# Two-layer block on one core: where the first norm's convolution taps, its gate and the local means are computed

## The chip, the cores and the metric

One core of one Trainium2 chip runs the whole program in one launch. The metric is device time in microseconds (us). Five engines run their own instruction queues in order: TensorE (PE for its products, PEld for its weight loads), VectorE (DVE), ScalarE (ACT), GpSimd (POOL), and SyncE (SP), whose queue issues nearly all DMA transfers here. Tiles lie in SBUF; TensorE writes its results to PSUM, eight banks of 512 fp32 columns on 128 partitions.

## The reference

Two layers act on x (1024 tokens by 1024 channels). Each takes h = rms(x) scaled and shifted by vectors made from c, puts it through a mixer, and adds the mixer's result times a gate vector to x. Layer 0 mixes by convolution, layer 1 by pooling:

```
a, b, g = split(h @ w_in, 3)                  # layer 0: 1024 -> 3 x 1024
y = a * sigmoid(b)
y = depthwise_conv(y, dw, 31 taps) + db       # along the tokens
y = silu(layernorm(y, ln_g, ln_b)) * silu(g)
x = x + gate * (y @ w_out)

v, g = split(h @ w_in, 2)                     # layer 1: 1024 -> 2 x 1024
pooled = window_mean(v, 2 | 4 | 8 | 16 by channel group) - v
y = (pooled @ w_grp) * scale                  # 4 groups of 256 channels
x = x + gate * ((y * silu(g)) @ w_out)
```

Everything is fp32. The tolerance is met by splitting each operand of a large product in two fp32r parts, hi (the rounded value) and lo (the rest), and summing three products (hi x hi, hi x lo, lo x hi).

## The kernel before

Channels lie on partitions, in eight tiles of 128 (ct, kt or m); tokens on columns, in two halves of 512 (h = 0, 1). A large product of one tile and half is 24 products (`mm3`, lines 202 to 205: three for each of eight input tiles) into one bank. `load_split` loads a weight tile of 512 KB, rounds it on ScalarE (`hi_part`, line 166) and takes the rest on VectorE or GpSimd (`lo_part`, line 171).

The order of work is: norm of x and modulation; for each channel tile a, b and y; the depthwise convolution of half 0; the gates silu(g) of half 0 (`gate_g`, stored to DRAM and read back); the norm of half 0 (`layernorm`), its SiLU and gating (`gate_norm`), the output product and residual (`out_half`), the second layer's input (`h2_half`); then layer 1 for part 0 of the tokens (the first 504; the rest is part 1) in four groups of two channel tiles (`layer1_group`), while the convolution of half 1 runs; then the same chain for half 1 and part 1.

The convolution has two forms. For tiles 1 and 3 of half 0 and 1, 3, 5, 6, 7 of half 1, ScalarE multiplies the input by a tap into a tile `pr` (line 468) and GpSimd adds it (line 469), 30 adds after a seed (line 465). For the others VectorE multiplies and adds tap by tap into two banks (lines 477, 481), summed at the end. In half 1 these are tiles 0, 2 and 4, in this order.

A planner fixes the order on each engine when the program is built. It runs the program on estimated durations, takes the ready instruction of the highest priority (by default the one created first; `priority(-LATER)` moves ahead, `conv` is put far behind), and honours three written orders: `behind([i])` queues what the block creates on i's own engine behind i; `ordered` puts an instruction behind the one created before it on its engine; and tiles of one tag get their slots in the order in which the code creates them. Banks come in three tags: mm (5), ax (1), cv (2).

What the change touches:

- The four modulation vectors (`gemv`, tag ax) advance in 16 steps; 7 are called between the a and b weights of tiles 4 to 7 (`MODS[0]`), 9 after the first three gates of half 0 (`MODS[1]`).
- `layernorm(0)` sums z over channels into a bank `mr` (mm in half 0, cv in half 1), spreads the mean into `mu` (ax), subtracts it on VectorE (line 542), squares on ScalarE (272) and sums the squares with TensorE into `vpz` (274). `rstd_rows` makes the power on GpSimd (240), a diagonal on ScalarE (245) and a spread bank `rb`.
- The convolution of tile 0 of half 1 is cut in pieces: `fill` creates 2 taps behind the mean, 3 behind the last subtraction, 1 and 3 in `rstd_rows` (`GAPS`); the other 22 are queued behind the last instruction of the gating. Tile 3 is queued behind the spread of the norm. Tile 2 has 8 taps behind the gating and the others behind the last instruction of h2.
- `gate_norm` scales a tile by `rb` (564, two tiles ahead), applies SiLU in place on ScalarE (567), multiplies by the gate (559), copies the rounded value (560) and subtracts it (171), all but the SiLU on VectorE and in SBUF.
- `window_mean` (part 0 and part 1) adds the value tile `v`, a copy of the product's bank, to itself shifted (671), doubles the window (675), corrects the edge on GpSimd (684), takes mean minus value (686) and splits it (166, 171).

Of the kernel before, what the change touches and what calls it, by code (L numbers as in the profile page):

```python
# [27 lines left out]
FILL = (4, 6, 5, 7)  # L28
EARLY = 8
MIX_AT = 4  # L30
# [4 lines left out]
HOLD = (4, 2, 3, 4)  # L35
GAPS = (2, 3, 1, 3)
LAST = 2
# [6 lines left out]
AFTER = mybir.DependencyInfo(mybir.DependencyClass.NoSync, mybir.DependencyReason.DATA)  # L44
MODS = ((1, 2, 2, 2), (3, 3, 3, 0, 0, 0))
CONVS = [
# [9 lines left out]
def hybrid_kernel(ctx, tc, xT, vecs, wm, wk, cv_first, cv_w, cv_wo, pl_w, pl_grp, pl_wo, out):  # L56
# [169 lines left out]

    def rstd_rows(total, name, fill=None):


        summed, vp = total  # L230
        if summed is not None:
            vp = axps(f"vp{name}")
            with priority(-LATER):
                for j in range(4):
                    nc.tensor.matmul(vp[:, j : j + 1], summed[:, bl(j)], ones[:, 0:1], start=True, stop=True)
        ve = S.tile([P, 4], F32, tag="ve", name=f"ve{name}", bufs=2)
        with priority(-LATER):
            scaled = nc.scalar.activation(ve, vp[:, 0:4], AF.Identity, scale=1.0 / D, bias=eps)  # L238
# [8 lines left out]
        if fill is not None:  # L247
            fill(GAPS[2], scaled)
            fill(GAPS[3], spread)
        spread_done[0] = spread  # L250
        return rb, done
# [15 lines left out]
    def square_sums(xs, name, vp):  # L267


        def add(i):  # L270
            sq = half("sq", f"sq{name}{i}")
            nc.scalar.activation(sq, xs[i], AF.Square)  # L272
            for j in range(4):
                last = nc.tensor.matmul(  # L274
                    vp[:, j : j + 1], sq[:, bl(j)], ones[:, 0:1], start=i + j == 0, stop=i == KT - 1,
                    skip_group_check=True,
                )
            return last

        return (None, vp), add  # L280
# [235 lines left out]

    for i, ct in enumerate((*FILL, *CORD[:2])):
        gate_g(ct, (0,) if ct in FILL else (0, 1))
        step(MODS[1][i])
    wg_last = {ct: gate_w(ct, 0) for ct in CORD[2:4]}  # L520
    for ct in CORD[2:4]:
        gate_g(ct, (0,), wg=wg_last[ct])

    sums_done = [None, None]

    def layernorm(h, banks, fill=None):
        z = [zs[h][ct] for ct in CORD]
        sums = bank(banks, f"mr{h}")
        row = S.tile([P, HW], F32, tag="row", name=f"mrow{h}", bufs=1)
# [7 lines left out]
        sums_done[h] = last  # L537
        if fill is not None:
            fill(GAPS[0], last)
        total, add = square_sums(z, f"z{h}", bank(banks, f"vpz{h}"))  # L540
        for i in range(KT):
            sub = nc.vector.tensor_tensor(out=z[i], in0=z[i], in1=mu, op=ALU.subtract)
            with priority(-LATER):
                add(i)
        if fill is not None:
            fill(GAPS[1], sub)
        return z, *rstd_rows(total, f"z{h}", fill)

    def gate_norm(h, z, rb):
# [7 lines left out]
        for i in range(-2, KT):  # L557
            if i >= 0:
                ordered(nc.vector.tensor_tensor(out=z[i], in0=z[i], in1=gates[i // 2][:, hs(i % 2)], op=ALU.mult))  # L559
                ordered(nc.vector.tensor_copy(y1[i][0], z[i]))  # L560
                end = ordered(lo_part(*y1[i], z[i]))
            if i + 2 < KT:
                ct, v = CORD[i + 2], z[i + 2]
                mul = nc.vector.tensor_tensor(out=v, in0=v, in1=rb, op=ALU.mult)  # L564
                if i > -2:
                    ordered(mul)
                last = nc.scalar.activation(v, v, AF.Silu, scale=vcol(ct, V_LG), bias=vcol(ct, V_LB))  # L567
        return y1, [last, end]
# [98 lines left out]

    def window_mean(ct, part, v, s):
# [17 lines left out]
        nc.vector.scalar_tensor_tensor(  # L686
            out=s, in0=s, scalar=1.0 / w, in1=v[:, PAD : PAD + n], op0=ALU.mult, op1=ALU.subtract
        )
        return split_to(*hi_lo(unit(f"Z{1 + ct % 2}", f"pd{ct}{part}", F32R, 2 * lo_at[part]), part), s)

    def layer1_group(g, part, h2, early=(), prev=None):
# [189 lines left out]
```

## Time and profile before

| | us |
|---|---|
| three runs | 807.47, 809.14, 805.24 (median 807.47) |
| profiled execution | 806.57, span 804.8 |
| TensorE busy | 736.9 (92%), 3564 products |
| VectorE busy | 588.6 (73%) |
| GpSimd busy | 421.4 (52%) |
| ScalarE busy | 380.4 (47%) |
| mean granted TensorE clock | 0.962 |

Busy shares are of the whole span and hide that the engines take turns: TensorE is near 20 of 20 us from 100 to 280 us, and VectorE and GpSimd have their full stretches between 310 and 560. A wait is listed as waiter, then what it waited for; a chain of waits is read from the end back. L481 is line 481.

### The profile page before, as it was taken

The page shows a single profiled execution, that of the slowest core. Times are in us where ns is not written, and L with a number is a line of the kernel's source. Part 1 is how long each engine was busy: PE and PEld are TensorE (multiplying, and loading weights), DVE is VectorE, ACT ScalarE, POOL GpSimd, SP SyncE. Part 2 cuts the span into 40 slices and gives each one's busy share as a digit, 9 for nine tenths or more (in the row PEclk, how much of TensorE's full clock was granted, in tenths as well). Part 3 has the DMA queues.
Part 4 walks back from the last instruction along what each step waited for, and adds up shares of the span by engine and source line. Part 5 has one row for each costly group of instructions (what it writes and reads, how often), then busy time and mean ns, then how long its engine had stood idle before and what let it go on. Part 6 is the DMA issues. An engine that isn't in the chain of part 4 may idle for free.

```text
span 804.8 us, 9866 instructions
## 1 busy us (share of the span) xinstructions
PE 736.9 (92%) x3564; PEld 582.9 (72%) x3564; DVE 588.6 (73%) x754; ACT 380.4 (47%) x560; POOL 421.4 (52%) x356
## 2 busy tenths in 40 slices
PE   3999999999999997699989768998899979999998
PEld 1677787777776675478767556775778758888998
DVE  6998997999994144999789999995285562666521
ACT  5446566566433225657766665752332442333210
POOL 2001899999400004879978989996121631444322
PEclk7899999999999997999999979899999989999999
DMA  9880022434268610343631222426432540233232
GB/s 338 321 293 23 1 72 112 158 111 171 86 210 316 219 53 26 119 157 117 198 104 40 79 91 80 133 91 234 156 118 104 185 142 1 92 106 130 79 108 80
DMA packets 36481, 105.68 MB, mean 131 GB/s; under 512 B 4048, under 2 KB 6224, under 8 KB 36432
## 3 DMA queue, kind: packets, MB, share of 16 engines
q1 hardware_dynamic: 36432, 105.05, 37.9%
q8 instruction: 28, 0.46, 0.2%
q14 instruction: 21, 0.17, 0.1%
HBM read 92.45 MB, written 12.58 MB: 131 GB/s over the span
## 4 chain that ended last, share of the span: by engine, by line
PE 56%; POOL 17%; DVE 11%; issue 7%; ACT 4%; DMA 4%; SPq 0%; POOLq 0%; ACTq 0%; DVEq 0%
POOL z L469 13%; PE ps L203 4%; PE ps L205 4%; PE ps L204 4%; PE psg L203 3%; PE psg L205 3%; PE psg L204 3%; PE psf L203 2%; PE pso L204 2%; PE psf L204 2%; PE psf L205 2%; PE pso L205 2%; PE pso L203 2%; PE psq L205 2%; PE gv L296 2%
## 5 line engine op out<-in xcount | busy, mean ns | idle before, releaser
L469 POOL TENSOR_TENSOR z<-z,pr 128x512 f32<-128x512 f32 (+8 forms) x210 | 311.5, 1484 | 49.6 <-ACT pr L468 21.9
L468 ACT ACTIVATE pr<-y,VT 128x512 f32<-128x512 f32 (+8 forms) x210 | 149.7, 719 | 101.4 <-POOL z L469 97.2
L481 DVE SCALAR_TENSOR_TENSOR cv<-y,VT,cv 128x512 f32<-128x512 f32 (+15 forms) x261 | 177.5, 742 | 0.2
L240 POOL TENSOR_TENSOR vrz<-vez,mhalf 128x4 f32<-128x4 f32 x2 | 2.0, 1018 | 122.2 <-ACT vez L238 122.2
L771 DVE SCALAR_TENSOR_TENSOR xf<-psf,gt,xf 128x260 f32<-128x260 f32 (+1 forms) x24 | 13.2, 570 | 40.8 <-PE psf L205 32.2
L671 DVE TENSOR_TENSOR s<-v 128x519 f32<-128x519 f32 (+1 forms) x16 | 21.8, 1362 | 19.4 <-ACT v L720 19.4
L754 DVE SCALAR_TENSOR_TENSOR q<-psy,VT,q 128x260 f32<-128x260 f32 (+1 forms) x24 | 13.4, 569 | 26.3 <-PE psy L205 26.2
L240 POOL TENSOR_TENSOR vrx<-vex,mhalf 128x4 f32<-128x4 f32 x2 | 2.1, 1026 | 56.5 <-ACT vex L238 56.5
L564 DVE TENSOR_TENSOR z<-z,rbz 128x512 f32<-128x512 f32 x16 | 10.7, 680 | 20.6 <-PE rbz L246 20.6
L675 DVE TENSOR_TENSOR s<-s 128x517 f32<-128x517 f32 (+5 forms) x24 | 23.1, 965 | 0.2
L567 ACT ACTIVATE z<-z,VT 128x512 f32<-128x512 f32 x16 | 12.8, 814 | 21.8 <-DVE z L564 21.8
L686 DVE SCALAR_TENSOR_TENSOR s<-s,v 128x504 f32<-128x504 f32 (+1 forms) x16 | 20.6, 1290 | 3.1 <-POOL s L684 2.9
L272 ACT ACTIVATE sqz<-z 128x512 f32<-128x512 f32 x16 | 10.0, 631 | 23.9 <-PE vpz L274 18.8
L171 DVE TENSOR_TENSOR y<-q,y 128x504 fp32r<-128x504 f32 (+1 forms) x16 | 17.4, 1090 | 3.7 <-ACT y L166 3.7
L284 DVE SCALAR_TENSOR_TENSOR wmb<-wmb,s_row 128x1024 f32<-128x1024 f32 x16 | 19.4, 1224 | 0.3 <-DMA wmb<-in_wm 0.3
L274 PEld LDWEIGHTS vpz<-ones,sqz 128*128 128x128 f32 x128 | 16.6, 204 | 2.4 <-ACT sqz L272 1.8
L513 ACT ACTIVATE sgw<-psg 128x512 f32<-128x512 f32 x16 | 9.5, 592 | 18.5 <-issue 11.1
L559 DVE TENSOR_TENSOR z<-z,sgr 128x512 f32<-128x512 f32 x16 | 17.3, 1080 | 1.0 <-ACT z L567 1.0
L296 PE MATMUL gv<-wk,srep 128*32 128x256 f32 x256 | 18.0, 386 | 0.0
L171 DVE TENSOR_TENSOR pd<-s,pd 128x504 fp32r<-128x504 f32 (+1 forms) x16 | 16.3, 1028 | 2.2 <-ACT pd L166 2.1
L166 ACT CAST y<-q 128x504 fp32r<-128x504 f32 (+1 forms) x16 | 9.8, 617 | 16.9 <-DVE q L754 16.8
L166 ACT CAST pd<-s 128x504 fp32r<-128x504 f32 (+1 forms) x16 | 9.8, 618 | 16.5 <-DVE s L686 12.1
(2496 smaller groups left out, 2385.4 us busy)
## 6 DMA issues: line engine op xcount, KB each, us to landing
wk<-in_wk SPq DMA_DIRECT2D x32, 512.0 KB, 5.3
wmb<-in_wm SPq DMA_DIRECT2D x16, 512.0 KB, 6.5
wo<-in_cv_wo SPq DMA_DIRECT2D x16, 512.0 KB, 4.2
wp<-in_pl_wo SPq DMA_DIRECT2D x16, 512.0 KB, 3.4
wg<-in_cv_w SPq DMA_DIRECT2D x12, 512.0 KB, 3.3
wv<-in_pl_w SPq DMA_DIRECT2D x12, 512.0 KB, 3.4
wq<-in_pl_w SPq DMA_DIRECT2D x12, 512.0 KB, 3.4
x<-in_xT SPq DMA_DIRECT2D x16, 256.0 KB, 6.4
```

Source lines behind the costliest of these rows:

```text
L166: return nc.scalar.copy(hi, src)
L171: return eng.tensor_tensor(out=lo, in0=src, in1=hi.bitcast(F32), op=ALU.subtract)
L203: nc.tensor.matmul(ps, w[0], r[0], start=first, stop=False)
L204: nc.tensor.matmul(ps, w[0], r[1], start=False, stop=False)
L205: nc.tensor.matmul(ps, w[1], r[0], start=False, stop=last)
L296: nc.tensor.matmul(ps[32 * q : 32 * q + 32, :256], srep[:, kt, :], w[:, 256 * q : 256 * q + 256], start=kt == 0, stop=kt == KT - 1,)
L468: nc.scalar.activation(pr[:, o], y[:, i], AF.Copy, scale=dw(k))
L469: nc.gpsimd.tensor_tensor(out=z[:, o], in0=z[:, o], in1=pr[:, o], op=ALU.add)
L481: nc.vector.scalar_tensor_tensor(out=a[:, o], in0=y[:, i], scalar=dw(k), in1=a[:, o], op0=ALU.mult, op1=ALU.add)
L671: nc.vector.tensor_tensor(out=s[:, :m], in0=v[:, :m], in1=v[:, 1 : m + 1], op=ALU.add)
L675: nc.vector.tensor_tensor(out=s[:, :m], in0=s[:, :m], in1=s[:, step : step + m], op=ALU.add)
L686: nc.vector.scalar_tensor_tensor(out=s, in0=s, scalar=1.0 / w, in1=v[:, PAD : PAD + n], op0=ALU.mult, op1=ALU.subtract)
```

## The change

Four edits. (1) All 16 modulation steps run between the weights of tiles 4 to 7; the mean's bank `mr` is of tag ax in both halves. (2) The convolutions of tiles 0, 1 and 2 of half 1 are created whole behind the gating with no written order; tile 3 is queued behind the last square of half 0 and no longer behind the spread. (3) The gating writes the SiLU to a bank of tag cv, multiplies there, rounds on ScalarE and subtracts on VectorE from the bank. (4) In part 0 the window sum takes one of its two inputs from the product's bank, the mean minus value is written over that bank, and the split reads it there; GpSimd clears seven columns of the sum tile first.

```diff
-MODS = ((1, 2, 2, 2), (3, 3, 3, 0, 0, 0))
@@ for ct in range(FIRST, KT):
     wb = load_split(cv_w[KT + ct], f"wb{ct}")
-    step(MODS[0][ct - FIRST])
+    step(2)
     wa = load_split(cv_w[ct], f"wa{ct}")
+    step(2)
@@ gates of half 0
     gate_g(ct, (0,) if ct in FILL else (0, 1))
-    step(MODS[1][i])
@@ layernorm
-    sums = bank(banks, f"mr{h}")
+    sums = axps(f"mr{h}")
-    total, add = square_sums(z, f"z{h}", bank(banks, f"vpz{h}"))
+    total, add = square_sums(z, f"z{h}", bank(("mm", "cv")[h], f"vpz{h}"))
+            squared[h] = add(i)      # the last square, on ScalarE
@@ gate_norm
-            ordered(nc.vector.tensor_tensor(out=z[i], in0=z[i], in1=gates[i // 2][:, hs(i % 2)], op=ALU.mult))
-            ordered(nc.vector.tensor_copy(y1[i][0], z[i]))
-            end = ordered(lo_part(*y1[i], z[i]))
+            b = bank("cv", f"gn{h}{i}")
+            last = nc.scalar.activation(
+                b, z[i], AF.Silu, scale=vcol(CORD[i], V_LG), bias=vcol(CORD[i], V_LB)
+            )
+            ordered(nc.vector.tensor_tensor(out=b, in0=b, in1=gates[i // 2][:, hs(i % 2)], op=ALU.mult))
+            hi_part(y1[i][0], b)
+            end = ordered(lo_part(*y1[i], b))
         if i + 2 < KT:
             mul = nc.vector.tensor_tensor(out=v, in0=v, in1=rb, op=ALU.mult)
             if i > -2:
                 ordered(mul)
-            last = nc.scalar.activation(v, v, AF.Silu, scale=vcol(ct, V_LG), bias=vcol(ct, V_LB))
@@ around the first norm
-early_taps = conv_taps(1, 0)
-def fill(count, ins):
-    with behind([ins]):
-        conv(1, 0, early_taps, count)
-z, rb, rb_done = layernorm(0, "mm", fill)
+z, rb, rb_done = layernorm(0)
...
-with behind(done[1:]):
-    conv(1, 0, early_taps)
-    conv(1, 1)
-    with behind(spread_done):
-        conv(1, 3)
-    taps = conv_taps(1, 2)
-    conv(1, 2, taps, EARLY)
+conv(1, 0)
+conv(1, 1)
+with behind([squared[0]]):
+    conv(1, 3)
+conv(1, 2)
...
         with behind([h2_done]):
-            conv(1, 2, taps)
             for ct in range(4, KT):
                 conv(1, ct)
@@ window_mean(ct, part, v, s, ps)
-    nc.vector.tensor_tensor(out=s[:, :m], in0=v[:, :m], in1=v[:, 1 : m + 1], op=ALU.add)
+    if part == 0:
+        nc.gpsimd.memset(s[:, : PAD - 1], 0.0)
+        nc.vector.tensor_tensor(out=s[:, PAD - 1 : m], in0=v[:, PAD - 1 : m], in1=ps, op=ALU.add)
+    else:
+        nc.vector.tensor_tensor(out=s[:, :m], in0=v[:, :m], in1=v[:, 1 : m + 1], op=ALU.add)
...
+    res, v = (ps[:, :n],) * 2 if part == 0 else (s, v[:, PAD : PAD + n])
+    nc.vector.scalar_tensor_tensor(out=res, in0=s, scalar=1.0 / w, in1=v, op0=ALU.mult, op1=ALU.subtract)
+    return split_to(*hi_lo(unit(f"Z{1 + ct % 2}", f"pd{ct}{part}", F32R, 2 * lo_at[part]), part), res)
```

## Rows read from the trace of the kernel before

**Rows 1.** The page's chain that ended last, by line.

```profile
POOL z L469 13%; PE ps L203 4%; PE ps L205 4%; PE ps L204 4%; PE psg L203 3%; PE psg L205 3%; PE psg L204 3%; PE psf L203 2%; PE pso L204 2%; PE psf L204 2%; PE psf L205 2%; PE pso L205 2%; PE pso L203 2%; PE psq L205 2%; PE gv L296 2%
```

**Rows 2.** Busy us by stage: length, PE, PEld, DVE, ACT, POOL; clock; DMA share, GB/s.

```profile
280.00:310.00 30.00, 26.02 (x138) 21.31 (x131) 9.49 (x15) 8.59 (x17) 1.02 (x1) 0.85 0.12 44
310.00:345.00 35.00, 24.73 (x82) 15.23 (x81) 31.93 (x32) 21.83 (x32) 27.57 (x19) 0.93 0.26 83
345.00:400.00 55.00, 54.30 (x259) 44.85 (x260) 48.03 (x54) 37.97 (x58) 48.58 (x31) 0.97 0.51 168
400.00:425.00 25.00, 21.18 (x84) 14.67 (x82) 22.41 (x20) 17.67 (x28) 19.68 (x16) 1.00 0.28 94
425.00:560.00 135.00, 115.85 (x466) 89.48 (x467) 123.36 (x129) 79.08 (x117) 122.62 (x96) 0.92 0.32 105
```

**Rows 3.** TensorE's waits, 425 to 560: us in total, times, longest.

```profile
PE psv L205 <- DVE wv40l L171: 7.0, 1, 7.0
```

**Rows 4.** Timeline of TensorE: start us, duration us, line, tiles; idle before, releaser.

```profile
279.10 1.92 PE L534 MATMUL mr<-z,onesd 128*32 128x512 f32 x16
...
294.63 1.84 PE L274 MATMUL vpz<-ones,sqz 128*128 128x1 f32 x16
...
300.33 1.84 PE L274 MATMUL vpz<-ones,sqz 128*128 128x1 f32 x16
...
303.05 3.88 PE L274 MATMUL vpz<-ones,sqz 128*128 128x1 f32 x24
...
548.67 1.05 PE L534 MATMUL mr<-z,onesd 128*32 128x512 f32 x4 [3.77 <-POOL z L469]
```

**Rows 5.** The page's costliest groups: busy us, mean ns; idle before.

```profile
L296 PE MATMUL gv<-wk,srep 128*32 128x256 f32 x256 | 18.0, 386 | 0.0
...
L166 ACT CAST pd<-s 128x504 fp32r<-128x504 f32 (+1 forms) x16 | 9.8, 618 | 16.5 <-DVE s L686 12.1
```

**Rows 6.** Timeline of VectorE around the gating of half 0.

```profile
291.99 4.70 DVE L481 SCALAR_TENSOR_TENSOR cv<-y,VT,cv 128x512 f32<-128x512 f32 x7
311.80 1.29 DVE L564 TENSOR_TENSOR z<-z,rbz 128x512 f32<-128x512 f32 x2 [15.12 <-PE rbz L246]
...
321.60 1.19 DVE L559 TENSOR_TENSOR z<-z,sgr 128x512 f32<-128x512 f32 x1
322.82 1.37 DVE L560 CAST y101h<-z 128x512 fp32r<-128x512 f32 x1
324.23 1.66 DVE L171 TENSOR_TENSOR y101l<-z,y101h 128x512 fp32r<-128x512 f32 x1
...
343.47 1.65 DVE L171 TENSOR_TENSOR y103l<-z,y103h 128x512 fp32r<-128x512 f32 x1
```

**Rows 7.** Timeline of VectorE in the gating of half 1.

```profile
599.05 0.43 DVE L560 CAST y112h<-z 128x512 fp32r<-128x512 f32 x1
599.51 0.69 DVE L171 TENSOR_TENSOR y112l<-z,y112h 128x512 fp32r<-128x512 f32 x1
```

**Rows 8.** Timeline of ScalarE at the start of the gating of half 0.

```profile
309.55 0.80 ACT L465 ACTIVATE z<-y,VT 128x512 f32<-128x512 f32 x1
...
312.97 1.50 ACT L567 ACTIVATE z<-z,VT 128x512 f32<-128x512 f32 x2
```

**Rows 9.** The chain that ended last, 353 to 400: start us, us, what.

```profile
353.00 0.23 PE pso L205
...
359.39 1.28 POOL z L469
...
392.04 2.16 POOL z L469
```

**Rows 10.** VectorE by line and form, 405 to 560: busy us, mean ns; idle before.

```profile
L686 DVE SCALAR_TENSOR_TENSOR s<-s,v 128x504 f32<-128x504 f32 x8 | 11.1, 1384 | 1.7 <-POOL s L684 1.6
L671 DVE TENSOR_TENSOR s<-v 128x519 f32<-128x519 f32 x8 | 9.5, 1186 | 0.0
L171 DVE TENSOR_TENSOR pd<-s,pd 128x504 fp32r<-128x504 f32 x8 | 9.1, 1133 | 0.7 <-ACT pd L166 0.7
```

More of the change, by code (lines that the diff above doesn't have):

```diff
@@ L28 @@
 FILL = (4, 6, 5, 7)
-EARLY = 8
 MIX_AT = 4
@@ L35 @@
 HOLD = (4, 2, 3, 4)
-GAPS = (2, 3, 1, 3)
 LAST = 2
@@ L225, in hybrid_kernel, with rstd_rows @@
     power_done, spread_done = [None], [None]
-    def rstd_rows(total, name, fill=None):
+    def rstd_rows(total, name):
         summed, vp = total
@@ L237, in rstd_rows @@
         with priority(-LATER):
-            scaled = nc.scalar.activation(ve, vp[:, 0:4], AF.Identity, scale=1.0 / D, bias=eps)
+            nc.scalar.activation(ve, vp[:, 0:4], AF.Identity, scale=1.0 / D, bias=eps)
         rs = S.tile([P, 4], F32, tag="vr", name=f"vr{name}", bufs=2)
@@ L246, in rstd_rows @@
             done = nc.tensor.matmul(rb, ones, dg, start=True, stop=True)
-        if fill is not None:
-            fill(GAPS[2], scaled)
-            fill(GAPS[3], spread)
         spread_done[0] = spread
@@ L271, in add @@
             sq = half("sq", f"sq{name}{i}")
-            nc.scalar.activation(sq, xs[i], AF.Square)
+            done = nc.scalar.activation(sq, xs[i], AF.Square)
             for j in range(4):
-                last = nc.tensor.matmul(
+                nc.tensor.matmul(
                     vp[:, j : j + 1], sq[:, bl(j)], ones[:, 0:1], start=i + j == 0, stop=i == KT - 1,
@@ L277, in add @@
                 )
-            return last
+            return done
         return (None, vp), add
@@ L515, in gate_g @@
             nc.sync.dma_start(out=sgd[h][i // 2][:, hs(i % 2)], in_=s)
-    for i, ct in enumerate((*FILL, *CORD[:2])):
+    for ct in (*FILL, *CORD[:2]):
         gate_g(ct, (0,) if ct in FILL else (0, 1))
-        step(MODS[1][i])
     wg_last = {ct: gate_w(ct, 0) for ct in CORD[2:4]}
@@ L522, in hybrid_kernel, with layernorm @@
         gate_g(ct, (0,), wg=wg_last[ct])
-    sums_done = [None, None]
-    def layernorm(h, banks, fill=None):
+    sums_done, squared = [None, None], [None, None]
+    def layernorm(h):
         z = [zs[h][ct] for ct in CORD]
-        sums = bank(banks, f"mr{h}")
+        sums = axps(f"mr{h}")
         row = S.tile([P, HW], F32, tag="row", name=f"mrow{h}", bufs=1)
@@ L537, in layernorm @@
         sums_done[h] = last
-        if fill is not None:
-            fill(GAPS[0], last)
-        total, add = square_sums(z, f"z{h}", bank(banks, f"vpz{h}"))
+        total, add = square_sums(z, f"z{h}", bank(("mm", "cv")[h], f"vpz{h}"))
         for i in range(KT):
-            sub = nc.vector.tensor_tensor(out=z[i], in0=z[i], in1=mu, op=ALU.subtract)
+            nc.vector.tensor_tensor(out=z[i], in0=z[i], in1=mu, op=ALU.subtract)
             with priority(-LATER):
[L544 to L547, printed above, removed]
+                squared[h] = add(i)
+        return z, *rstd_rows(total, f"z{h}")
     def gate_norm(h, z, rb):
@@ L558, in gate_norm @@
             if i >= 0:
-                ordered(nc.vector.tensor_tensor(out=z[i], in0=z[i], in1=gates[i // 2][:, hs(i % 2)], op=ALU.mult))
-                ordered(nc.vector.tensor_copy(y1[i][0], z[i]))
-                end = ordered(lo_part(*y1[i], z[i]))
+                b = bank("cv", f"gn{h}{i}")
[5 more added lines that the diff above has]
+                end = ordered(lo_part(*y1[i], b))
             if i + 2 < KT:
-                ct, v = CORD[i + 2], z[i + 2]
+                v = z[i + 2]
                 mul = nc.vector.tensor_tensor(out=v, in0=v, in1=rb, op=ALU.mult)
@@ L666, in hi_lo, with window_mean @@
         return u[:, : count[part]], u[:, lo_at[part] : lo_at[part] + count[part]]
-    def window_mean(ct, part, v, s):
+    def window_mean(ct, part, v, s, ps):
         w, n = 2 << (ct // 2), count[part]
         m = n + 2 * PAD - 1
-        nc.vector.tensor_tensor(out=s[:, :m], in0=v[:, :m], in1=v[:, 1 : m + 1], op=ALU.add)
+        if part == 0:
[3 more added lines that the diff above has]
+            nc.vector.tensor_tensor(out=s[:, :m], in0=v[:, :m], in1=v[:, 1 : m + 1], op=ALU.add)
         step = 2
@@ L685, in window_mean @@
         s = s[:, b : b + n]
[L686 to L689, printed above, removed]
+        res, v = (ps[:, :n],) * 2 if part == 0 else (s, v[:, PAD : PAD + n])
+        nc.vector.scalar_tensor_tensor(out=res, in0=s, scalar=1.0 / w, in1=v, op0=ALU.mult, op1=ALU.subtract)
+        return split_to(*hi_lo(unit(f"Z{1 + ct % 2}", f"pd{ct}{part}", F32R, 2 * lo_at[part]), part), res)
     def layer1_group(g, part, h2, early=(), prev=None):
@@ L725, in layer1_group @@
             layer1_mix(*prev)
-        pd = [window_mean(2 * g + j, part, vs[j], sums[:, j * wide : (j + 1) * wide]) for j in range(2)]
+        pd = [window_mean(2 * g + j, part, vs[j], sums[:, j * wide : (j + 1) * wide], psv[j]) for j in range(2)]
         gate = unit("Z3", f"q{g}{part}", cols=WIDTH["Z"])
@@ L811, in hybrid_kernel @@
     with priority(-LATER):
-        z, rb, rb_done = layernorm(1, "cv")
+        z, rb, rb_done = layernorm(1)
     layer1_out(0, range(MID_OUT - 1), ahead, group)
```

## The prediction

> **What bounds the kernel now.** I read the chain of waits first, then busy time by stage, then the waits of TensorE, then the orders of the engines around the first norm. The page's chain names TensorE lines in shares of 2 to 4% and one line that is not TensorE: GpSimd's convolution adds, 13% [rows 1]. TensorE is busy 737 of 804.8 us, so what a change can win is what is left of the difference. By stage it lies in three places. From 280 to 310 TensorE is idle 4.0 us (30 less 26.02), from 310 to 345 10.3 us (35 less 24.73), from 425 to 560 19.2 us (135 less 115.85) [rows 2]. The second place is the gating of half 0: VectorE works 31.9 of 35 us there and TensorE waits for it. In the third, VectorE (123 of 135) and GpSimd (123 of 135) are both full; TensorE waits for weight splits queued late on VectorE, 7.0 us at the longest [rows 3], and at 548.67 3.77 us for GpSimd's last convolution add [rows 4]. That add releases the norm of half 1, from which everything behind hangs.
>
> **The profiled execution** took 806.57 us (span 804.8, 1.8 around it), 0.9 below the median of 807.47. The sum is made against 806.57 and 0.9 is added at the end.
>
> **Part 1: the first norm.** Today the sums of half 0 (mr) run at 279.10 although their last input is done long before: their bank is of tag mm, and banks of a tag are given out in the order of creation, here behind the last gate bank of half 0, whose first product stands just ahead of mr. The change puts mr in ax, which is free once the last modulation vector is made; with all 16 steps of these vectors moved into the loop before, that is earlier. The moved steps cost TensorE the same work in another place. They push the last convolution inputs back by 9 of the 16 steps, some 10 us (all 16 are 18.0 [rows 5]), and the last VectorE convolution of half 0 by no more; its mean is then taken off by about 270 instead of 292 [rows 6], well ahead of the next gate. That gate is the bank of the squares (vpz0), still mm: it opens where mr stands today plus some 3 us for mr (1.92 [rows 4]) and mu, which move ahead of it: 282. From there four pairs of column sums follow. Spaced 5.7 us as today (294.63 to 300.33 [rows 4]) the last ends at 301; spaced by their own 1.84 us and two squares, some 3 us, at 293. From that end to VectorE's first product it was 4.9 us (303.05 plus 3.88 to 311.80 [rows 4, 6]). So the gating starts between 298 and 306 instead of 311.8; I take 303. Gate products of half 1 that ran before it are then filler during it.
>
> **Part 2: the gating.** Today a tile costs VectorE a product with the gate, a copy, a subtraction and the next tile's scaling: 1.19 + 1.37 + 1.66 + 0.65 beside a GpSimd add [rows 6], and less when GpSimd is idle, 0.43 and 0.69 for copy and subtraction [rows 7]. From 311.8 to 345.1 [rows 6] this is 33.3 us, 4.2 a tile. After the change VectorE does three operations with one input in a bank. The nearest row is the scaling, which reads rb from a bank: 0.65 in the same loop, where the copy takes three times what it takes alone [rows 6]. The rounding goes to ScalarE, whose cast of such a tile took 0.62 [rows 5], and it stands inside the loop: product, cast, subtraction, scaling. 0.65 x 3 + 0.62 + two handovers of 0.1 = 2.8 a tile, 22 for eight, 24 with the first SiLU (0.75 each [rows 8]). Bounds: 2.0 if the cast were hidden, 4.2 as today if ScalarE's convolution products (pr) stand ahead of the casts. I take 2.8, and the gating ends at 327 instead of 345.1. TensorE then still has nine products (2.1 us at 0.23 [rows 9]) of the first output group and loses some 2.5 us to the lower granted clock (0.93 in this stage [rows 2]): 332 instead of 346, **14 us earlier** (bounds 4 and 20). Its own work fits: three gate banks of 24, 72 output products, the column sums and rb are some 42 us from 282 on, 324.
>
> In half 1 GpSimd is idle during the gating, a tile costs 2.4 us today, and TensorE needs twelve products, 2.8 us, for each. At 2.8 us the new loop is level with it; I charge 0.5 us. The row of the copy, 0.43 against 0.69 for the subtraction [rows 7], shows what is given up here. The Trainium skill says the same against this change (VectorE: DVE Perf Modes, "Why PSUM operands drop a tier"): an operand in PSUM caps an fp32 operation at the basic rate. By that rule alone, with no gain elsewhere, half 1 would lose 0.4 us a tile, 3 us; the row agrees on the copy.
>
> **Part 3: the convolutions of half 1.** In spite of the name, the ones on VectorE are not free to start: their cv banks are created behind the eight that the gating now takes. The nine taps that ran ahead of the gating, seven of them in 4.70 us at 292 [rows 6], move behind it, 9 x 0.67 = 6 us, into VectorE time that the shorter loop gave up (11 us there), so they cost nothing unless the loop stays long. The one on GpSimd that waited for the spread of the norm (seed at 309.55 [rows 8]) now waits for the last square only, about 299: GpSimd, busy 1.0 of 30 us before 310 [rows 2], starts 10 us earlier, and beside VectorE work with a bank operand its adds during the gating run shorter (as in part 4). I put its lead at 345 at 14 us.
>
> **Part 4: local means.** Of eight tiles of part 0 three operations each get a bank operand: 1.19, 1.38 and 1.13 us [rows 10] become 0.68 to 0.74, some 12.8 us of VectorE between 425 and 560 (bounds 0 and 13). ScalarE reads a bank instead of SBUF, nothing. Eight tiny memsets on GpSimd come in. The value banks stay held until the differences are split; the next group's mix waits for these anyway, so no new wait; if that cover fails, a bank costs the length of the local means, several us a group. VectorE gets room for the late weight splits: of TensorE's 19.2 us idle in these groups 3.8 are the wait for the add; of the other 15.4 it wins back 8. GpSimd's adds took 1.28 us alone and 2.16 beside VectorE work with two SBUF inputs [rows 9]; of the 24 operations that stop being such, I count nine such delays, 8 us, less 2 for tiny work.
>
> **The sum.** At the sums of half 1 TensorE would be 14 + 8 = 22 us ahead, GpSimd's last add 14 + 6 = 20. The later one sets the norm: 20, of which I take 18, since the weight splits ahead of the last adds on GpSimd may stay where they are. Behind that the work is unchanged but for the 0.5. 806.57 - 18 + 0.5 + 0.9 = 789.97, **790 us**, own range 782 to 799.
>
> **Rivals.**
> *GpSimd does not move.* ScalarE serves both the loop and GpSimd's products; if the casts, waiting for VectorE, hold up the pr behind them, the adds during the gating fall back and the last add comes only 5 us earlier. TensorE, though ahead, waits there. For it: its chain has that line as the largest [rows 1]. Against it: before 303 GpSimd has ScalarE nearly to itself. 806.57 - 5 + 0.9 = 802.
> *The port is worth more.* If all 24 operations had delayed an add by 0.9 us, GpSimd gains 21, not 8, and VectorE's lateness goes entirely: TensorE wins 14 in the gating and all 19.2 of the groups: 806.57 - 33.2 + 0.9 = 774. Against it: the weight splits, which remain, cause the long runs of 2.16 us adds. The Trainium skill (SBUF — State Buffer, "Who interferes with whom") states that a VectorE instruction with at most one SBUF input does not contend with GpSimd while one with two does; by that rule this rival would come out. The rows of the scaling and of the two adds agree with it [rows 6, 9].
> *Slower: the second VectorE convolution in the way of h2.* Its last 23 taps were held behind h2 and now are not. The stage from 400 to 425 is paced by VectorE (22.4 of 25 us busy) with TensorE behind it [rows 2]. Each tap put between its steps delays it by 0.67 us. From 27 taps on the 18 us are gone; at 35, 23.5 us, the time is 806.57 + 23.5 - 18 + 0.9 = 813. For it: the planner fills a VectorE that it believes idle. Against it: from 327 to h2 there are about 60 us, some 27 of them other work (48.0 busy from 345 to 400 [rows 2] less 31 taps), so 50 of the 62 taps fit ahead of it.
>
> **Chances.** Forecast 0.55, GpSimd unmoved 0.17, port 0.14, slower 0.14. Within 0.5% (4 us), about what a measurement can tell, lie the upper part of the first rival and the edge of the last. Faster by over 0.5%: 0.78; within: 0.10; slower: 0.12. The range for 8 in 10 takes in the first two rivals and the edge of the third: 772 to 809.
>
> **What would show it.** Right: first gating product at about 303; tiles 2.8 us apart; first output group ended by 332; GpSimd's adds beginning before 300 and ending before 532; the sums of half 1 and the rest 18 us earlier. Wrong: gating tiles still 4 us apart (pr ahead of the casts), the last add after 540, cv taps between the steps of h2, or TensorE waiting for a bank of tag mm in the four groups.

## The result and the profile after

The changed kernel takes **776.63 us** (median of 4 runs, 774.19 to 777.52) against 807.71 (4 runs, 805.24 to 809.14): ratio 0.9614, 95% interval 0.9581 to 0.9646. Predicted were 790, range 772 to 809. The profiled execution took 776.93, span 775.1, 29.7 less than before. TensorE's busy time fell from 736.9 to 727.3 us and its idle time (span less busy) from 67.9 to 47.8: 9.6 and 20.0 us make up the difference.

The page's first rows and its chain by line, after:

```profile
PE 727.3 (94%) x3564; PEld 573.9 (74%) x3564; DVE 548.0 (71%) x738; ACT 387.2 (50%) x576; POOL 409.4 (53%) x364
...
PE psf L201 3%; PE psf L202 3%; PE psf L200 3%; PE psv L200 2%; PE psq L200 2%; PE psv L201 2%; PE psv L202 2%; PE psq L202 2%; PE psq L201 2%; PE pso L201 1%; PE pso L200 1%; PE pso L202 1%; DMA we<-in_pl_w 1%; DMA wv<-in_pl_w 1%; PE vpz L268 1%; PE psy L200 1%
```

GpSimd's add, 13% of the chain before [rows 1], is gone from it. Busy time by stage (columns as in [rows 2]); the third stretch of before, 425 to 560, is here 425 to 530:

```profile
280.00:310.00 30.00, 28.64 (x155) 23.76 (x153) 2.37 (x4) 14.95 (x27) 10.19 (x9) 1.00 0.20 71
310.00:345.00 35.00, 30.61 (x133) 22.60 (x134) 27.21 (x39) 28.36 (x45) 32.21 (x24) 1.00 0.50 161
345.00:400.00 55.00, 48.42 (x227) 38.12 (x225) 51.38 (x60) 42.16 (x64) 52.54 (x35) 1.00 0.46 148
400.00:425.00 25.00, 24.71 (x98) 19.02 (x99) 24.89 (x31) 15.40 (x24) 23.00 (x19) 0.93 0.13 45
425.00:530.00 105.00, 98.22 (x432) 76.17 (x431) 89.80 (x103) 68.50 (x103) 90.68 (x85) 0.98 0.40 132
530.00:560.00 30.00, 30.00 (x142) 24.75 (x142) 16.05 (x25) 12.75 (x22) 4.77 (x3) 1.00 0.48 156
```

TensorE is idle 1.4 us in the first stage (4.0 before), 4.4 in the second (10.3), 6.8 in the four groups (19.2), but 6.6 from 345 to 400, where it had been idle 0.7 [rows 2]: there VectorE is now full (51.4 of 55), and TensorE comes into the stage some 14 us further on in its work. Timeline of TensorE, as [rows 4]:

```profile
283.89 1.84 PE L268 MATMUL vpz<-ones,sqz 128*128 128x1 f32 x16
289.58 1.84 PE L268 MATMUL vpz<-ones,sqz 128*128 128x1 f32 x16
295.27 1.84 PE L268 MATMUL vpz<-ones,sqz 128*128 128x1 f32 x16
...
501.95 1.05 PE L528 MATMUL mr<-z,onesd 128*32 128x512 f32 x4
...
556.93 0.39 PE L202 MATMUL psf<-y,wp50l 128*128 128x504 f32 x1
557.16 0.40 PE L200 MATMUL pso<-y110h,wo10h 128*128 128x512 f32 x1
```

The sums of half 1 (mr) come 46.7 us earlier than in [rows 4] and TensorE is not idle before them, yet the first output product of half 1 (pso) comes only 32 us earlier (before at 589.42), right behind the products called feedforward in this text (psf): layer 1's output product for part 0, which needs nothing of half 1. Timeline of VectorE in the gating of half 0, as [rows 6]:

```profile
306.75 1.28 DVE L558 TENSOR_TENSOR z<-z,rbz 128x512 f32<-128x512 f32 x2 [26.36 <-PE rbz L243]
308.29 0.70 DVE L553 TENSOR_TENSOR gn<-gn,sgr 128x512 f32<-128x512 f32 x1 [0.26 <-ACT gn L550]
310.11 0.69 DVE L168 TENSOR_TENSOR y100l<-gn,y100h 128x512 fp32r<-128x512 f32 x1 [1.12 <-ACT y100h L163]
310.71 0.68 DVE L558 TENSOR_TENSOR z<-z,rbz 128x512 f32<-128x512 f32 x1
311.31 0.69 DVE L553 TENSOR_TENSOR gn<-gn,sgr 128x512 f32<-128x512 f32 x1
313.01 0.69 DVE L168 TENSOR_TENSOR y100l<-gn,y100h 128x512 fp32r<-128x512 f32 x1 [1.01 <-ACT y100h L163]
...
331.11 0.69 DVE L168 TENSOR_TENSOR y103l<-gn,y103h 128x512 fp32r<-128x512 f32 x1
```

All three operations take 0.68 to 0.70 us; about 1 us a tile is the wait for ScalarE's cast. And the local means, VectorE by line and form (as [rows 10]), each 0.67 to 0.68 us where it was 1.13 to 1.38:

```profile
L676 DVE SCALAR_TENSOR_TENSOR psv<-s,psv 128x504 f32<-128x504 f32 x8 | 5.4, 679 | 0.4 <-POOL s L673 0.3
L658 DVE TENSOR_TENSOR s<-v,psv 128x512 f32<-128x512 f32 x8 | 5.4, 676 | 0.0
L168 DVE TENSOR_TENSOR pd<-psv,pd 128x504 fp32r<-128x504 f32 x8 | 5.4, 669 | 0.0
```

GpSimd: the first add of half 1 starts at 299.2 (before 311.0), the last ends at 501.8 (before 548.6).

### The profile page after: what moved, and what is told of

Same layout as the page of the kernel before. It is cut to its first block, busy times and chain, and to the rows that moved or that the text cites. A ratio compares the mean times of both kernels' runs of the same rounds, so it can differ in the third digit from the quotient of the medians.

```text
span 775.1 us, 9869 instructions
## 1 busy us (share of the span) xinstructions
PE 727.3 (94%) x3564; PEld 573.9 (74%) x3564; DVE 548.0 (71%) x738; ACT 387.2 (50%) x576; POOL 409.4 (53%) x364
## 5 line engine op out<-in xcount | busy, mean ns | idle before, releaser
L463 POOL TENSOR_TENSOR z<-z,pr 128x512 f32<-128x512 f32 (+8 forms) x210 | 303.4, 1446 | 123.7 <-ACT pr L462 95.0
L475 DVE SCALAR_TENSOR_TENSOR cv<-y,VT,cv 128x512 f32<-128x512 f32 (+12 forms) x261 | 177.4, 742 | 0.3
L742 DVE SCALAR_TENSOR_TENSOR q<-psy,VT,q 128x260 f32<-128x260 f32 (+1 forms) x24 | 13.5, 569 | 36.9 <-PE psy L202 36.8
L558 DVE TENSOR_TENSOR z<-z,rbz 128x512 f32<-128x512 f32 x16 | 10.7, 678 | 30.5 <-PE rbz L243 30.5
L660 DVE TENSOR_TENSOR s<-v 128x535 f32<-128x535 f32 x8 | 12.3, 1538 | 20.6 <-ACT v L708 20.6
L574 DVE SCALAR_TENSOR_TENSOR xr<-pso,gt,xr 128x512 f32<-128x512 f32 x16 | 11.6, 743 | 14.0 <-PE pso L202 13.5
L550 ACT ACTIVATE gn<-z,VT 128x512 f32<-128x512 f32 x16 | 12.2, 773 | 12.8 <-DVE z L558 12.8
L603 DVE SCALAR_TENSOR_TENSOR xr<-xr,a,rby 128x512 f32<-128x512 f32 x16 | 11.6, 737 | 7.9 <-PE rby L243 7.9
L168 DVE TENSOR_TENSOR y<-q,y 128x504 fp32r<-128x504 f32 (+1 forms) x16 | 14.1, 884 | 3.9 <-ACT y L163 3.9
L201 PE MATMUL psy<-pd,grs 128*128 128x260 f32 (+1 forms) x48 | 15.3, 320 | 1.5 <-DVE pd L168 1.5
L268 PEld LDWEIGHTS vpz<-ones,sqz 128*128 128x128 f32 x128 | 15.4, 192 | 1.2 <-ACT sqz L266 0.6
L202 PE MATMUL psy<-pd,grs 128*128 128x260 f32 (+1 forms) x48 | 15.3, 319 | 0.0
L200 PE MATMUL psy<-pd,grs 128*128 128x260 f32 (+1 forms) x48 | 15.1, 321 | 0.0
L268 PE MATMUL vpz<-ones,sqz 128*128 128x1 f32 x128 | 14.8, 246 | 0.2 <-ACT sqz L266 0.2
```

Of the source, the lines that this page charges most:

```text
L168: return eng.tensor_tensor(out=lo, in0=src, in1=hi.bitcast(F32), op=ALU.subtract)
L200: nc.tensor.matmul(ps, w[0], r[0], start=first, stop=False)
L201: nc.tensor.matmul(ps, w[0], r[1], start=False, stop=False)
L202: nc.tensor.matmul(ps, w[1], r[0], start=False, stop=last)
L268: nc.tensor.matmul(vp[:, j : j + 1], sq[:, bl(j)], ones[:, 0:1], start=i + j == 0, stop=i == KT - 1, skip_group_check=True,)
L463: nc.gpsimd.tensor_tensor(out=z[:, o], in0=z[:, o], in1=pr[:, o], op=ALU.add)
```

## The experiments

Idle and busy are TensorE's in the profiled execution; "last add" is the end of GpSimd's last convolution add. "low clock" is how many us between 30 and 760 of that execution TensorE's granted clock was at the lower of its two levels (1.2 of 2.4 GHz). Ratios are to the kernel before, run on the same chip. The profiled execution lies over 2 us from the median in three kernels: u_gate (785.12, the slowest of four), r_dve (780.91, the slowest of five) and better (767.94, the fastest of six, the others 772.4 to 773.4).

| kernel | median us | ratio, 95% interval | idle | busy | last add | low clock |
|---|---|---|---|---|---|---|
| before | 807.71 | | 67.9 | 736.9 | 548.6 | 47.8 |
| changed | 776.63 | 0.9614 (0.9581 to 0.9646) | 47.8 | 727.3 | 501.8 | 13.7 |
| u_gate | 782.08 | 0.9675 (0.9629 to 0.9720) | 51.3 | 732.0 | 515.8 | 23.9 |
| u_means | 785.07 | 0.9718 (0.9681 to 0.9756) | 51.1 | 732.9 | 510.7 | 30.7 |
| u_front | 786.36 | 0.9739 (0.9697 to 0.9781) | 54.1 | 730.5 | 509.4 | 30.7 |
| u_conv | 771.63 | 0.9557 (0.9520 to 0.9594) | 44.2 | 727.1 | 514.3 | 10.2 |
| s_hold | 776.31 | 0.9613 (0.9574 to 0.9652) | 44.2 | 731.2 | 502.5 | 23.9 |
| s_seed | 776.76 | 0.9617 (0.9576 to 0.9657) | 46.4 | 728.4 | 511.3 | 17.1 |
| g_slow18 | 792.07 | 0.9795 (0.9740 to 0.9850) | 51.8 | 739.0 | 502.3 | 41.0 |
| b_means | 795.60 | 0.9854 (0.9811 to 0.9897) | 59.9 | 734.6 | 537.3 | 37.5 |
| b_slow6 | 814.70 | 1.0089 (1.0060 to 1.0118) | 68.9 | 744.3 | 546.9 | 58.0 |
| r_dve | 778.08 | 0.9644 (0.9614 to 0.9673) | 45.2 | 734.0 | 505.0 | 30.7 |
| better | 772.77 | 0.9576 (0.9546 to 0.9606) | 38.7 | 727.5 | 502.4 | 13.7 |
| best | 765.06 | 0.9480 (0.9450 to 0.9510) | 38.2 | 724.9 | 513.8 | 6.8 |

The columns busy and low clock go together: from best to b_slow6 the time at the lower clock grows by 51.2 us and the busy time by 19.4, 0.38 us for each, and every other kernel lies within 4 us of that line, for the same 3564 products.

**u_gate**, the gating back in SBUF:

```
- b = bank("cv", ...); last = activation(b, z[i], Silu); b *= gate; hi_part(y, b); lo_part(y, b)
+ z[i] *= gate; vector.tensor_copy(y_hi, z[i]); lo_part(y, z[i])    # SiLU in place, two tiles ahead
```

> The gating goes back to SBUF (product in place, VectorE's copy and subtraction); all else stays as in the changed kernel. With the cv banks free again, 62 VectorE taps of half 1 are queued ahead of the gating. Order theory (the loop's length and its start are what counts): a tile takes about 4 us instead of 3.1, the first output group of TensorE ends some 10 us later than its 329 us, and 8 to 12 us of that stay in the time: 785 to 789 us. Port theory (operations with two SBUF inputs lengthen GpSimd's adds): beside that, the 16 operations with two SBUF inputs cost GpSimd up to 0.9 us each, its mean add up to 345 us goes back from 1.37 to 1.52 us, its last add comes over 12 us later than 502 us and the time is 790 us or more. If the gating is worth nothing: 777 us.

A tile took 3.8 us (low part to low part), the first output group ended at 342.4 instead of 333.2, GpSimd's mean add up to 345 rose from 1.37 to 1.49 us, and its last add came 14 us later: both theories' signs, but 5 us by the medians instead of 8 to 12 (or over 13). The two intervals together leave about 0 to 9, and the profiled execution lost 8, so the size is not well known. A part of the 9.2 us at the first output group came back behind it, as the busy time by stage shows:

```profile
280.00:310.00 30.00, 28.94 (x156) 24.00 (x155) 27.74 (x43) 15.84 (x28) 10.21 (x9) 1.00 0.21 73
345.00:400.00 55.00, 54.51 (x268) 44.99 (x267) 26.86 (x21) 39.57 (x60) 50.62 (x33) 1.00 0.50 167
```

With the cv banks free, VectorE does some 50 tap operations between 266 and 308 (27.7 of 30 us busy from 280, where the changed kernel has 2.4) and has only 26.9 of 55 us left to do from 345 to 400; TensorE is idle 0.5 us there instead of 6.6, in part because it comes into the stage 9.2 us behind and has more work left. From the end of the first output group to the first value product of layer 1 it needs 60.2 us (342.4 to 402.6) against 63.2 in the changed kernel (333.2 to 396.4): by work done, the banks that the gating now takes cost some 3 us there, half of what the window shows.

**u_means**, local means of part 0 back in SBUF:

```
- s[:, PAD-1:m] = v[:, PAD-1:m] + ps;  res, v = ps, ps      (part 0)
+ s[:, :m] = v[:, :m] + v[:, 1:m+1];   res, v = s, v        (both parts)
```

> Local means of part 0 back in SBUF, all else as in the changed kernel. Prediction's part 4 (12.8 us of VectorE, 8 of them on TensorE's path): TensorE's idle time in the four groups grows from 7 us to about 15, time 784 us (781 to 787). Port theory: GpSimd's mean add from 425 us on rises from 1.51 us towards 1.56 or more, its last add comes 10 us later or more and TensorE waits for it at the sums of half 1. Clock theory (TensorE's idle stretches pull the granted clock down, which takes a part of its own): TensorE's busy time rises by 3 us or more beside the idle time, and the groups' clock falls from 0.98 towards 0.92. If VectorE's work in the groups is hidden: 777 us.

8.4 us, as predicted, by another split: idle grew by 3.2 us and busy by 5.6. The wait and the stage that show it:

```profile
PE psv L202 <- DVE wv40l L168: 6.5, 1, 6.5
```

```profile
425.00:530.00 105.00, 94.05 (x393) 72.23 (x391) 100.14 (x104) 66.95 (x99) 92.96 (x78) 0.95 0.34 113
```

VectorE is 10 us busier in the groups and the late weight split of [rows 3] is back (0.3 us in the changed kernel); the adds from 425 on take 1.64 us on average instead of 1.51; the granted clock there is 0.95 instead of 0.98. All three theories have a part; but TensorE does not wait longer than 1 us for an add, though the last one comes 9 us later.

**u_front**, the modulation steps and the bank of mr as before:

```
- sums = axps(f"mr{h}")
+ sums = bank(("mm", "cv")[h], f"mr{h}")       # and step() back behind the first three gates
```

> Only the first norm's front undone: the steps of the modulation vectors stand where they were and the sums of half 0 take a bank of tag mm again. Prediction's part 1: the bank of the squares opens some 10 us later than 284, the gating starts at about 311 instead of 307 us, and 4 to 8 us stay in the time: 781 to 785 us. Rival (the start of the gating is paced by something else, the shorter loop and freer GpSimd have slack for it): 777 to 779 us.

The gating started at 311.78 instead of 306.75, the first output group ended 6.6 us later, and 9.7 us were lost, more than expected: idle 6.2, busy 3.2.

**u_conv**, both written orders of the convolutions back:

```
- with behind([squared[0]]): conv(1, 3)        - conv(1, 2)
+ with behind(spread_done):  conv(1, 3)        + conv(1, 2, taps, 8)  ...  behind h2: conv(1, 2, taps)
```

> The written orders of two convolutions of half 1 back: GpSimd's third one waits for the spread of the norm, and VectorE's second one is held behind h2 after 8 taps. GpSimd starts some 10 us later and its last add comes at about 512 instead of 502 us. Theory that TensorE sets the end and GpSimd has 8 to 13 us of slack: 777 to 780 us. Rival, the prediction's sum (the later of the two sets the norm, and it is GpSimd): 786 us.

Neither: it is **faster**, 771.3 to 773.2 us in its runs against 774.2 to 777.5. GpSimd's last add came 12.5 us later and cost nothing. VectorE in the changed kernel and then here, at the end of h2 (its low parts are L169):

```profile
417.05 1.38 DVE L475 SCALAR_TENSOR_TENSOR cv<-y,VT,cv 128x504 f32<-128x504 f32 x2
418.35 0.74 DVE L169 SCALAR_TENSOR_TENSOR h206l<-xr,sh,h206h 128x512 fp32r<-128x512 f32 x1
419.01 0.73 DVE L475 SCALAR_TENSOR_TENSOR cv<-y,VT,cv 128x502 f32<-128x502 f32 x1
419.66 1.12 DVE L169 SCALAR_TENSOR_TENSOR h206l<-xr,sh,h206h 128x512 fp32r<-128x512 f32 x1
```

```profile
410.83 2.81 DVE L169 SCALAR_TENSOR_TENSOR h206l<-xr,sh,h206h 128x512 fp32r<-128x512 f32 x2
413.57 7.32 DVE L475 SCALAR_TENSOR_TENSOR cv<-y,VT,cv 128x512 f32<-128x512 f32 x11
```

Ten tap operations (7.3 us) between the first and the last step of h2 in the changed kernel, one here; h2 is done at 413.6 instead of 420.8. The slower rival's mechanism is real.

**s_hold** and **s_seed**, each of these orders alone (the diff's right and left half):

> The changed kernel with one written order back: VectorE's second convolution of half 1 does 8 taps and holds its other 23 behind h2; GpSimd's third convolution stays free to start. If the 5 us that both orders back gained come from the 9 taps between the steps of h2 (9 x 0.67 = 6 us on VectorE, the mechanism of the prediction's slower rival), this one gives them alone: 770 to 773 us, the end of the last group's value product 3 to 5 us earlier, and no cv taps between the steps of h2. If they come from GpSimd's later start: 776 to 778 us.

> The other half: GpSimd's third convolution of half 1 waits again for the spread of the norm, the taps stay free. If the taps are the cause of the 5 us: 776 to 778 us, with GpSimd's last add some 10 us later than 502 us and nothing lost by it. If the start of GpSimd is the cause: 770 to 773 us.

s_hold did what the tap theory says (h2 done at 413.4, idle 3.6 us less) and gained nothing, because TensorE's busy time rose by 3.9 us; s_seed lost nothing by a last add 9.5 us later. So GpSimd's start is not the cause, and the taps alone don't make the 5 us. In s_hold the clock is 0.92 from 560 to 620:

```profile
560.00:620.00 60.00, 52.76 (x225) 41.87 (x223) 30.52 (x33) 22.68 (x33) 19.11 (x10) 0.92 0.45 148
```

against 0.97 in the changed kernel and 0.95 in u_conv. Over the span it is 23.9 us at the lower clock, against 13.7 and 10.2; an estimate from the spacing of products in g_slow18 (0.42 us at the lower clock, 0.23 at the higher; rows in the last section): 10.2 us more of it cost up to 4.6, enough for the 3.9. So the lost time is the clock's; why it stays up with both orders and not with one is open.

**g_slow18** and **b_slow6**, extra work right behind GpSimd's last add, in the changed kernel and in the kernel before:

```
+ for _ in range(18):      # 6 in b_slow6
+     gpsimd.tensor_tensor(out=z7, in0=z7, in1=ones, op=mult)     # last tile of half 1
```

> The changed kernel with 18 extra GpSimd products right behind its last convolution add (the last tile of half 1 times ones, so values stay), some 1.3 us each, 24 us in all: the sums of half 1 come at about 526 instead of 502 us and the gating at 568 instead of 544. TensorE sets the end (its feedforward products run to 557 us, so there are some 13 us of slack): +11 us, 784 to 791 us. Rival, the prediction's sum (GpSimd's last add sets the norm): +24 us, 798 to 802 us. If more is hidden than the slack seen: under 780 us.

> The kernel before with 6 extra GpSimd products right behind its last convolution add (the last tile of half 1 times ones, so values stay), 1.3 to 1.6 us each, 8 to 10 us in all. The prediction's premise (the last add sets the norm of half 1 and all behind hangs from it): +8 to +10 us, 816 to 818 us. Theory that TensorE's own stream, with its idle stretches, sets the time in the kernel before too (its feedforward products run on to 590 us, past the norm): +0 to +4 us, 807 to 812 us.

In both the planner let weight splits of GpSimd slip between the extra products, so the sums moved further than planned. Timeline of TensorE in g_slow18, then its busy time by stage:

```profile
545.83 1.05 PE L528 MATMUL mr<-z,onesd 128*32 128x512 f32 x4 [1.85 <-POOL z L800]
...
550.13 13.81 PE L268 MATMUL vpz<-ones,sqz 128*128 128x1 f32 x64 [1.44 <-ACT sqz L266]
```

```profile
530.00:560.00 30.00, 26.03 (x115) 21.50 (x113) 10.62 (x15) 6.62 (x10) 15.15 (x11) 0.83 0.47 166
560.00:620.00 60.00, 57.24 (x241) 46.53 (x242) 31.89 (x40) 25.52 (x38) 17.29 (x10) 0.91 0.33 110
```

The sums came **44 us later, the end 15.4**: the changed kernel has some 28 us of slack there. A good part of it is the norm itself, which takes 42.4 us from its sums to the gating (501.95 to 544.35) when other products stand between its steps, and 23.0 here (545.83 to 568.82), where 129 of these 144 products are done ahead of it. What is lost is 4.0 us idle and 11.7 us of longer busy time, with the clock at 0.83 and 0.91 where the changed kernel has 1.00 and 0.97 at these times. In b_slow6 they came 14.2 us later:

```profile
562.90 1.92 PE L534 MATMUL mr<-z,onesd 128*32 128x512 f32 x4 [2.82 <-POOL z L813]
```

```profile
425.00:560.00 135.00, 119.60 (x490) 93.16 (x488) 121.04 (x124) 77.17 (x114) 127.01 (x99) 0.95 0.33 108
560.00:650.00 90.00, 81.25 (x345) 65.31 (x345) 50.75 (x65) 30.02 (x42) 24.66 (x14) 0.88 0.38 128
```

and it took 7.2 us longer (interval 4.8 to 9.5): idle 1.0, busy 7.4. TensorE waited 2.8 us for the add, less than the 3.77 of [rows 4], since it had done 106 feedforward products ahead of it instead of 48. Both expectations were made for a delay of 8 to 10 us, and neither range holds 7.2; for the 14.2 that it became, the prediction's premise would have cost 14. So even before the change the last add did not simply set the time: half of a delay was hidden, and the other half was paid mostly at the lower clock. The kernel before, from 560 to 650, has 0.96 where b_slow6 has 0.88:

```profile
560.00:650.00 90.00, 81.45 (x380) 66.79 (x378) 48.55 (x64) 31.09 (x46) 25.72 (x13) 0.96 0.46 154
```

**b_means**, the local means in PSUM as the only edit to the kernel before (u_means' diff the other way round):

> The kernel before with the local means of part 0 in PSUM and nothing else of the change. Prediction's part 4: GpSimd 6 us earlier, TensorE 8 us in the groups, and the later of them sets the norm: 802 us (800 to 804). Port theory (24 operations with two SBUF inputs less, up to 0.9 us of a GpSimd add each): GpSimd's mean add from 425 us falls from 1.56 towards 1.3 us, its last add comes 15 us or more earlier and the time is 792 to 796 us. If the groups were paced otherwise: 807 us.

-12.5 us by the run's own before of 808.07 (8 to 15 by the interval), past the prediction's part 4 and at the port theory's time by another way: idle fell by 8.0 us (in the groups by 9.4, of which 3.8 are the wait for the add, gone here), the last add came 11.3 us earlier (the prediction's 6), the adds from 425 on took 1.47 instead of 1.56 us, not 1.3.

**r_dve**, the gated tile rounded by VectorE:

```
- hi_part(y1[i][0], b)                               # ScalarE
+ ordered(nc.vector.tensor_copy(y1[i][0], b))
```

> The changed kernel with the gated tile rounded by VectorE out of the bank instead of by ScalarE. By the rows of the changed kernel a tile has VectorE work of some 2.0 us beside the handovers to ScalarE and its cast of 0.57; a copy out of the bank at about the 0.65 of the scaling takes their place, so a tile stays near 3 us. If ScalarE's casts matter only through the length of the loop: 775 to 779 us. If taking them from VectorE is what freed GpSimd and the groups: 780 us or more, with the first output group at 340 instead of 333 us.

Timeline of VectorE, one tile:

```profile
313.80 0.69 DVE L553 TENSOR_TENSOR gn<-gn,sgr 128x512 f32<-128x512 f32 x1
314.53 0.69 DVE L554 CAST y101h<-gn 128x512 fp32r<-128x512 f32 x1
315.25 0.69 DVE L168 TENSOR_TENSOR y101l<-gn,y101h 128x512 fp32r<-128x512 f32 x1
315.86 0.68 DVE L558 TENSOR_TENSOR z<-z,rbz 128x512 f32<-128x512 f32 x1
```

A tile takes 2.7 us, less than the 3.0 with ScalarE's cast, and the gating ends 2 us earlier; idle time falls by 2.6 us, busy time rises by 6.7 (in the slowest of its runs, with 30.7 us at the lower clock), and the median is 778.1, not told apart from the change. ScalarE's rounding brought nothing that can be measured.

**better** and **best**: in the changed kernel TensorE's longest wait is 6.6 us for the spread of half 1's second norm (rby), whose diagonal and power stand behind the cast and the split of one weight that arrives late. The edit, alone and with u_conv's:

```
- with behind([h2_started] if part == 0 and ct == 2 else []):
+ with behind([h2_started] if part == 0 and ct == 2 else
+             [power_done[0], spread_done[0]] if part and ct == 2 else []):
      w = load_split(pl_w[ct], f"wv{ct}{part}", ...)
```

> The changed kernel with one weight (value layer, third tile, part 1) queued behind the power and the spread of half 1's second norm. Today TensorE waits 6.6 us at that spread: ScalarE's diagonal stands behind the cast of this weight, whose transfer ends late, and GpSimd's power behind its split. If that order is the cause: the wait falls under 2 us and the time to 769 to 773 us. If the spread is late for another reason, or the weight's lateness comes back at its own products: 776 to 778 us.

> Both convolution orders of half 1 as they were before, and that weight queued behind the spread as well. If the gains of the two add: 5 us from each, 765 to 768 us. If, as for the two convolution orders, where TensorE's idle time goes shifts its granted clock and a part is given back: 769 to 773 us.

The wait in the changed kernel, in better and in best:

```profile
PE rby L243 <- ACT dgy L242: 7.6, 2, 6.6
```

```profile
PE rby L243 <- ACT dgy L242: 1.5, 1, 1.5
```

```profile
PE rby L243 <- ACT dgy L242: 0.5, 1, 0.5
```

Better takes 772.77 us, **best 765.06** (764.76 to 765.41), ratio 0.948 (0.945 to 0.951), 11.6 us below the change: the two gains add (5.0 and 3.9 alone; the 2.7 beyond their sum is within the noise of four medians). And its page's chain by line begins so:

```profile
POOL z L463 18%; PE ps L200 4%; PE ps L202 4%; PE ps L201 4%; PE psf L200 3%; PE psf L201 3%; PE psf L202 3%; PE psg L200 3%; PE psg L202 3%; PE psg L201 3%; PE gv L290 2%; PE psv L201 2%; PE psq L200 2%; PE psv L200 2%; PE psq L202 2%
```

GpSimd's add has a larger share of the chain than in the kernel before, in the fastest kernel of all. It also has 13% in s_hold and 18% in s_seed, which take the time of the changed kernel, where it has none. In best its slack is used up: ScalarE casts the first gated tile of half 1 until 554.3, and TensorE starts on it at 554.65, straight from its feedforward products. It costs no wait yet; no run delays the add there.

## Why the prediction was right, and where it was wrong

The direction and the range held; the time was missed by 13 us. Lead of the changed kernel over the one before, by TensorE's rows (the last add by GpSimd's):

| point | before | after | lead | predicted |
|---|---|---|---|---|
| bank of the squares opens | 288.6 | 283.9 | | at 282 |
| first gating product | 311.8 | 306.8 | 5.0 | 8.8 |
| first output group ends (72nd output product) | 347.1 | 333.2 | 13.9 | 14 |
| first value product of layer 1 | 407.1 | 396.4 | 10.7 | |
| last product of the fourth group | 532.8 | 511.7 | 21.1 | 22 |
| last add of GpSimd | 548.6 | 501.8 | 46.8 | 20 |
| first output product of half 1 | 589.4 | 557.2 | 32.2 | 18 |

- **Part 1**, right in kind: the bank opened at 283.9, the pairs of sums are 5.7 us apart as in [rows 4], the gating starts at 306.8, 3.8 later than taken and 0.8 past the bound.
- **Part 2**: a tile takes 3.0 us (low part to low part; 3.8 before), where 2.8 was taken; the cast is inside the loop as reckoned. 13.9 us against 14 is luck in part: the gating ended at 331.8, 4.8 later than the 327 taken, and TensorE needed 1.4 us behind it instead of 5, since the clock of this stage was 1.00 and the 2.5 us charged for it did not come. The Trainium skill's rule against it (VectorE: DVE Perf Modes, "Why PSUM operands drop a tier") holds by the row of the copy: 0.69 us out of a bank in r_dve against 0.43 out of SBUF [rows 7]. Its loss in half 1 can't be seen, because TensorE comes to those products later than VectorE.
- **Part 3**: "they cost nothing unless the loop stays long" was wrong. The taps that the taken banks push behind the gating fill VectorE from 345 to 400, and the lead falls from 13.9 to 10.7 (TensorE is idle 5.9 us more in that window, in part because it gets there sooner); ten tap operations then stand inside h2. u_gate, with 3 us, and u_conv bear this out.
- **Part 4**: the three operations went from 29.7 to 16.2 us, 13.5 against 12.8 predicted. Of the 15.4 us that TensorE was idle in the groups beside the wait for the add, b_means alone wins back 5.6 and the whole change 8.6, where 8 was taken. The adds of half 1 took 180.6 us instead of 188.3, 7.7 against the 8 predicted.
- **The step that failed** is in the sum: "The later one sets the norm: 20", with "Behind that the work is unchanged". TensorE stood where the sum put it (21.1 for 22), but GpSimd's last add came 47 us earlier, not 20. Its start gave 11.8 and the adds 7.7, as predicted; 8.5 came from three weight splits that now run behind the last add instead of ahead of it, 2.1 from smaller work and 16.7 from idle time between the adds, none of which is in the sum. And the last add did not set the time: it still releases the sums of half 1, but so early that the norm runs beneath TensorE's feedforward products; the first gated tile is there at 549.0, and TensorE gets to it at 557.2. From the last product of the groups to half 1's first output product TensorE needed 56.6 us before (7.3 idle, of which 3.8 waiting for the add and 2.8 for the spread), and 45.5 after, where it idles for 0.2:

```profile
512.00:557.00 45.00, 44.83 (x221) 37.40 (x220) 19.71 (x31) 17.92 (x30) 15.51 (x10) 0.96 0.55 175
```

  These 11 us are most of the miss of 13. Three more are the 18 taken where TensorE led by 21, and 2 went back behind that product: to the end it is 218.0 us against 215.4 before, where 0.5 was charged, mostly longer waits at the second norm of half 1 (6.6 and 1.4 us, 5.8 before). u_conv, s_seed and g_slow18 show that the add has slack after; b_slow6 shows that it had some before.
- **The clock** was charged 2.5 us in one place; over the whole span TensorE's busy time fell by 9.6 for the same 3564 products, with 13.7 us at the lower clock instead of 47.8. In u_gate, u_means, u_front and g_slow18 a third to three quarters of what is lost against the change is busy time.

Of the rivals, "the port is worth more" gave the nearest time (774) for a wrong reason: the adds gained 8 us, not 21. Its rule itself holds row by row in the changed kernel. Of the 120 adds of half 1 in the changed kernel, 52 ran with no VectorE operation on two SBUF tensors beside them and took 1.28 us on average, 1.31 at most, whatever else VectorE did; 50 that overlapped one by over 0.6 us took 1.76. The Trainium skill says so (SBUF — State Buffer, "Who interferes with whom"), and this trace agrees. One input is no safe sign by itself, though: in the kernel before the copy, with one SBUF input, took 1.37 us beside an add and 0.43 alone [rows 6, 7]. And what an add is worth is another question: here it was little.

## What to carry to other kernels

When one engine is busy over 90% of the span, work in its idle time and its clock, not in the lead of another engine: the last add moved 47 us and was worth 11 at most, and in the fastest kernel it comes 12 us later than in the changed one. A line's share in the chain of waits is no price (13%, none, 18% at 807, 777 and 765 us here); add a known delay behind the suspect and see what part of it arrives. And when a tile moves into a bank of a shared tag, ask which older user of that bank now runs later, and in whose way.

## What was not expected of the hardware

A gain of idle time can come back as busy time: s_hold saved 3.6 us of TensorE's idle time and lost 3.9 to longer products, with 23.9 us at the lower clock instead of 13.7; g_slow18 paid 11.7 of 15.4 us so. The granted clock of a stage is a mean over its two levels (1.2 and 2.4 GHz), and fell to 0.83 (g_slow18, 530 to 560) where TensorE had run out of feedforward products and did the short, waiting ones of the norm. The feedforward products behind them start 0.42 us apart at the lower level and 0.23 at the higher:

```profile
569.42 0.62 PE L202 MATMUL psf<-y,wp50l 128*128 128x504 f32 x1
569.84 0.62 PE L200 MATMUL psf<-y,wp50h 128*128 128x504 f32 x1
...
571.00 0.39 PE L201 MATMUL psf<-y,wp50h 128*128 128x504 f32 x1
571.23 0.40 PE L202 MATMUL psf<-y,wp50l 128*128 128x504 f32 x1
```
